# Two of the seven lower parts of a Strassen pair: negated copy and accumulating DMA in place of a VectorE subtraction

## The chip, the cores and the metric

The kernel runs on one core of one Trainium2 chip (trn2). The metric is the device time of one execution in microseconds (us). A core has five engines that run side by side, each with its own queue worked off in order: TensorE (PE in the profile; PEld is its weight load), VectorE (DVE), ScalarE (ACT), GpSimd (POOL) and SyncE (SP), which here only starts DMAs. They wait for one another through semaphores. DMAs move data between the DRAM arrays and the on-chip memory.

## The reference

One inference step of a two-layer encoder over 512 prompt frames and 64 sample frames, model width 1024. Layer 0 mixes tokens by causal pooling, layer 1 by sparse attention; each is followed by a squared-ReLU MLP with 4096 hidden units. All data is float32. What matters here is the MLP:

```python
def _mlp(h, w_up, w_down):
    u = jax.nn.relu(h @ w_up)
    return (u * u) @ w_down
```

It is computed once in each layer, on the 576 frames together.

## The kernel before

**Split weights.** TensorE multiplies in float32r, a shortened float32. To keep accuracy, each weight block is split into an upper part h (the block rounded to float32r) and a lower part l (the block minus h), and each activation likewise; a product is then three matmuls: h by h, h by the activation's lower part, l by h. `split_unit` (L176 to L180) makes a *unit*, the two parts of a block of 128 x 512: ScalarE copies the block into the tile `wh` (L178), VectorE subtracts into `wl` (L179).

**Rings.** Units stand in a ring of six buffers plus, in the MLP, two more (`UNITS`, L39), so eight. The raw blocks come from DRAM by DMAs of 512 KB (`load`, L142 to L145; issued by SyncE in the MLP) into a ring of two plus two buffers (`RAWS`, L41). `loaded` (L182) keeps up to three loads ahead. `next_unit` (L219) makes units up to five ahead of the one that TensorE takes next.

**Stages of an MLP.** The hidden units are worked in four quarters c = 0 to 3. For each quarter there is an up stage (`project`, matmuls at L253, tile `up`), and a down stage. The down stage of a quarter below `strassen` (four quarters in layer 0, three in layer 1) uses a form of Strassen's algorithm with seven products in place of eight: four pairs of output tiles in each of the seven quarters, 28 pairs in all (`Pair`, L387 to L423, tiles `a`, `b`, `c`, matmuls at L384). The last quarter of layer 1 is done without it (tile `dn`).

**A pair's seven half blocks.** Each pair loads two raw blocks, of kinds "even" and "odd"; the even one holds the half blocks a11 and a12, the odd one a21 and a22, each 128 x 512. `made` (L192 to L215) turns them into seven units, in this order: a11; s2 = a21 + a22 + a11; s1 = a21 + a22; a12; a21 + a11; s2 + a12; a22. The sums are made by GpSimd (L205, L206, L210, L213), in place where they can be. So a11, a12 and a22 are split as they come from DRAM; the others exist only on chip. The opening of a pair takes the first three units, the closing the other four; one unit is 12 matmuls. VectorE adds the products to the residual `x` (L409 to L411, L423). In the last Strassen quarter of a layer GpSimd also adds the running sum `g` onto the residual (L414 to L416). The activations' own factors `u` are made by VectorE and ScalarE in `factors` (L363 to L377).

**What sets the order.** Each engine's queue is put in order by a planner that works from its own model of durations and readiness and from the program's order as priority; in the stages around the change nothing is ordered by hand. Waits follow from what an instruction reads and writes, and from a buffer's last readers.

Of the kernel before, what the change touches and what calls it, by code (L numbers as in the profile page):

```python
# [11 lines left out]
AF = mybir.ActivationFunctionType  # L12
ALU = mybir.AluOpType
# [35 lines left out]
def pool_dsa_kernel(ctx: ExitStack, tc: tile.TileContext, a, o):  # L49
    nc = tc.nc  # L50
    act, dve, pool, pe = nc.scalar, nc.vector, nc.gpsimd, nc.tensor
# [11 lines left out]
    def uid(s):  # L63
        count[0] += 1
        return f"{s}_{count[0]}"
# [37 lines left out]
    def f32(t):  # L103
        return t.bitcast(F32)
# [26 lines left out]
    def longer(what, sizes, mlp):  # L131

        if not (mlp and "more" in phase):
            return False
        t, turns[what] = turns[what], turns[what] + 1
        return t * sizes[1] // sum(sizes) != (t + 1) * sizes[1] // sum(sizes)

    def raw_tile(mlp=False):
        pool = phase["more"] if longer("raw", RAWS, mlp) else raws
        return pool.tile([P, 4 * 264], F32, tag="raw", name=uid("raw"))  # L140

    def load(src, n, queue, mlp=False):  # L142
        raw = raw_tile(mlp)
        queue.dma_start(raw[:, :n], src)
        return raw  # L145
# [25 lines left out]
    def unit(n=512, mlp=False):  # L171

        pool = phase["more"] if longer("unit", UNITS, mlp) else weights
        return [pool.tile([P, 528], F32R, tag=t, name=uid(t))[:, :n] for t in ("wh", "wl")]

    def split_unit(src, mlp):  # L176
        h, l = unit(src.shape[1], mlp)
        act.copy(h, src)  # L178
        how["sub"].tensor_tensor(l, src, f32(h), ALU.subtract)  # L179
        return h, l  # L180

    def loaded():  # L182

        waiting = []
        while jobs or waiting:
            while jobs and len(waiting) < LOADS_AHEAD["more" in phase]:
                kind, src, n = jobs.pop(0)
                mlp = kind in MLP_BLOCKS
                waiting.append((kind, load(src, n, nc.sync if mlp else act, mlp)[:, :n], mlp))
            yield waiting.pop(0)  # L190

    def made():  # L192

        blocks = loaded()
        for kind, raw, mlp in blocks:
            if kind != "even":
                n = raw.shape[1] // 2
                for i in range(2):  # L200
                    yield split_unit(raw[:, i * n:(i + 1) * n], mlp)
                continue
            a11, a12, a21, a22 = (t[:, i * 512:(i + 1) * 512] for t in (raw, next(blocks)[1]) for i in range(2))
            s1, s2 = (phase["sums"].tile([P, 512], F32, tag="sum", name=uid("sum")) for _ in range(2))
            pool.tensor_tensor(s1, a21, a22, ALU.add)  # L205
            pool.tensor_tensor(s2, s1, a11, ALU.add)  # L206
            yield split_unit(a11, mlp)
            yield split_unit(s2, mlp)
            yield split_unit(s1, mlp)
            pool.tensor_tensor(a21, a21, a11, ALU.add)  # L210
            yield split_unit(a12, mlp)
            yield split_unit(a21, mlp)
            pool.tensor_tensor(s2, s2, a12, ALU.add)  # L213
            yield split_unit(s2, mlp)
            yield split_unit(a22, mlp)  # L215

    units = made()

    def next_unit(ahead=4, sub=dve):  # L219
# [1039 lines left out]
```

## Time and profile before

| | before |
|---|---|
| median of 3 runs | 1127.58 us (1126.56 to 1128.9) |
| profiled execution, span from first to last instruction | 1125.7 us (its own time; no other figure of it is given) |
| TensorE busy | 1095.9 us (97%), 8254 matmuls |
| VectorE busy | 823.0 us (73%), 1493 instructions |
| ScalarE busy | 537.4 us (48%), 971 instructions |
| GpSimd busy | 336.0 us (30%), 257 instructions |
| DMA traffic | 114.33 MB, 102 GB/s on average |
| TensorE's mean granted clock | 0.987 of full |

The profile is of one execution. A group's row gives line, engine, operation, tiles and shape, the count, then busy us and mean ns of one, and after the second bar the engine's idle time just before and what ended it. A row of a timeline gives the start and the duration in us, and in brackets the idle time before it. A row of waits gives the waiting engine and line, what ended the wait, the total in us, the number of waits and the longest one. Matmuls are pipelined, so a matmul's own duration (295 ns) is longer than the step from one to the next.

### The profile page before, as it was taken

Reading aid. Unit: us, or ns where it says so; the run is one execution under the profiler, and the core shown is the slowest. Engines: PE = TensorE matmul, PEld = TensorE weight load, DVE = VectorE, ACT = ScalarE, POOL = GpSimd, SP = SyncE. Lnnn points to the kernel's source line nnn. Section 1 sums busy time; section 2 is a strip of 40 time slices with the busy share of each in tenths; the row PEclk is TensorE's granted clock in tenths of the full one; section 3 lists DMA queues with packets and bytes.
Section 4 is the critical chain, followed back from the end, with each engine's and each line's share of the span. In section 5 each row is a group of like instructions: output and inputs, shape, how many; then the busy total and the mean of one; then the engine's idle time right before and its main releaser. Section 6 shows DMA issues by size and latency. Waiting matters only on the chain.

```text
span 1125.7 us, 20859 instructions
## 1 busy us (share of the span) xinstructions
PE 1095.9 (97%) x8254; PEld 1083.3 (96%) x8254; DVE 823.0 (73%) x1493; ACT 537.4 (48%) x971; POOL 336.0 (30%) x257
## 2 busy tenths in 40 slices
PE   8999999999999999999799999999999999999995
PEld 8999999999999999999789999999999999999995
DVE  7878857867786797569999944778858867774434
ACT  8544444344434455354387765545434434433431
POOL 3223212403123361157962430023202403350002
PEclk9999999999999999999899999999999999999998
DMA  6221431331232135457632442421331242242202
GB/s 218 97 76 38 115 112 57 95 128 60 76 116 91 39 117 168 131 157 197 178 101 68 134 142 83 145 77 39 113 113 57 90 128 65 59 129 95 76 1 85
DMA packets 47185, 114.33 MB, mean 102 GB/s; under 512 B 8449, under 2 KB 20016, under 8 KB 47088
## 3 DMA queue, kind: packets, MB, share of 16 engines
q1 hardware_dynamic: 42336, 95.66, 27.7%
q10 hardware_dynamic: 4752, 17.34, 4.8%
q8 instruction: 65, 1.06, 0.4%
q14 instruction: 32, 0.26, 0.1%
HBM read 97.90 MB, written 10.89 MB: 97 GB/s over the span
## 4 chain that ended last, share of the span: by engine, by line
PE 90%; DVE 5%; ACT 1%; DMA 1%; issue 1%; POOL 1%; SPq 0%; DVEq 0%; ACTq 0%; POOLq 0%
PE up L253 36%; PE b L384 11%; PE c L384 7%; PE a L384 7%; PE pj L253 7%; PE dn L253 4%; PE o L1015 3%; PE wo L253 3%; PE wa L253 2%; PE sc L976 1%; PE v L809 1%; PE pb L744 1%; PE pt L996 1%; DVE wl L179 1%; DVE work L940 1%; PE o L1019 1%
## 5 line engine op out<-in xcount | busy, mean ns | idle before, releaser
L253 PE MATMUL up<-xs,wh 128*128 128x288 f32 x2048 | 355.2, 295 | 3.9 <-DVE v L355 2.6
L178 ACT CAST wh<-raw 128x512 fp32r<-128x512 f32 (+1 forms) x322 | 197.9, 620 | 300.3 <-PE up L253 115.5
L253 PEld LDWEIGHTS up<-xs,wh 128*128 128x128 f32 x2048 | 299.5, 188 | 5.4 <-DVE v L355 3.5
L179 DVE TENSOR_TENSOR wl<-raw,wh 128x512 fp32r<-128x512 f32 (+1 forms) x298 | 235.2, 792 | 72.7 <-ACT wh L178 67.5
L253 PE MATMUL up<-xs,wl 128*128 128x288 f32 x1024 | 218.7, 295 | 0.0
L205 POOL TENSOR_TENSOR sum<-raw 128x512 f32<-128x512 f32 x28 | 40.7, 1454 | 483.2 <-DMA raw<-in_w_down 406.0
L253 PEld LDWEIGHTS up<-xs,wl 128*128 128x128 f32 x1024 | 164.0, 188 | 0.0
L384 PE MATMUL b<-u,wh 128*128 128x288 f32 x672 | 135.8, 295 | 0.4 <-DVE u L376 0.2
L384 PEld LDWEIGHTS b<-u,wh 128*128 128x128 f32 x672 | 107.5, 188 | 0.8 <-DVE u L376 0.4
L178 ACT CAST wh<-sum 128x512 fp32r<-128x512 f32 x84 | 51.4, 620 | 100.5 <-PE up L253 34.3
L384 PE MATMUL b<-u,wl 128*128 128x288 f32 x336 | 98.8, 295 | 0.0
L384 PE MATMUL a<-u,wh 128*128 128x288 f32 x448 | 92.7, 297 | 2.0 <-DVE u L375 2.0
L355 DVE SCALAR_TENSOR_TENSOR v<-up,rbm 128x576 f32<-128x576 f32 x62 | 46.6, 755 | 65.4 <-PE up L253 64.8
L384 PE MATMUL c<-u,wh 128*128 128x288 f32 x448 | 91.1, 295 | 0.0
L179 DVE TENSOR_TENSOR wl<-sum,wh 128x512 fp32r<-128x512 f32 x84 | 79.9, 955 | 4.8 <-ACT wh L178 3.8
L253 PE MATMUL pj<-xs,wh 128*128 128x288 f32 x448 | 78.9, 295 | 0.0
L384 PEld LDWEIGHTS a<-u,wh 128*128 128x128 f32 x448 | 72.9, 190 | 2.3 <-DVE u L375 2.3
L384 PEld LDWEIGHTS c<-u,wh 128*128 128x128 f32 x448 | 71.9, 188 | 0.0
L253 PEld LDWEIGHTS pj<-xs,wh 128*128 128x128 f32 x448 | 66.6, 188 | 0.7
L384 PE MATMUL a<-u,wl 128*128 128x288 f32 x224 | 66.4, 296 | 0.0
L384 PE MATMUL c<-u,wl 128*128 128x288 f32 x224 | 66.1, 295 | 0.0
L356 ACT ACTIVATE v<-v 128x576 f32<-128x576 f32 x64 | 43.9, 687 | 46.1 <-DVE v L355 45.7
(223 smaller groups left out, 2067.1 us busy)
## 6 DMA issues: line engine op xcount, KB each, us to landing
raw<-in_w_up SPq DMA_DIRECT2D x64, 512.0 KB, 3.5
raw<-in_w_down SPq DMA_DIRECT2D x64, 512.0 KB, 3.5
raw<-in_w_o ACTq DMA_DIRECT2D x16, 512.0 KB, 3.7
raw<-in_w_in ACTq DMA_DIRECT2D x15, 512.0 KB, 3.9
q<-st SPq DMA_DIRECT2D x32, 144.0 KB, 3.3
q<-q SPq DMA_DIRECT2D x16, 256.0 KB, 2.9
x<-in_x SPq DMA_DIRECT2D x8, 288.0 KB, 6.2
xd<-x SPq DMA_DIRECT2D x4, 576.0 KB, 3.0
```

The costliest lines, as they stand in the source:

```text
L178: act.copy(h, src)
L179: how["sub"].tensor_tensor(l, src, f32(h), ALU.subtract)
L205: pool.tensor_tensor(s1, a21, a22, ALU.add)
L253: pe.matmul(pt[h][:, :m] if isinstance(pt, tuple) else pt[:, h, :m], wt, xs[k][:, part, c:c + m], start=(k == 0 and i == 0), stop=(k == n ...
L355: dve.scalar_tensor_tensor(v, pt[:, :, :HT], 0.0, halves(norm.rb), ALU.max, ALU.mult)
L356: act.activation(v, v, AF.Square)
L384: pe.matmul(bank[:, :HT], wt, ut, start=first and j == 0 and i == 0, stop=last and j == 3 and i == 2, skip_group_check=True)
L744: pe.matmul(pt[:, c0:c0 + rhs.shape[1]], lhs, rhs, start=n == 0, stop=n == len(steps) - 1)
L809: pe.matmul(pt[:n, :264], xs[k][:, part, i * P:i * P + n], wt[:, sl], start=(k == 0 and j == 0), stop=(k == KT - 1 and j == 2))
L940: dve.match_replace(wk[:np_], m8[:np_], wk[:np_], TAKEN)
L976: pe.matmul(pt[:, hh, :nw], q[:, 2 * s + hh], ks[g][:, part, :nw], start=part == 0, stop=part == 1)
L1015: pe.matmul(oc[:, 2 * s + hh], pT[:, c:c + P], V[:, kt, vs], start=kt == 0, stop=kt == i)
```

## The change

For a12 and a22 a new function, `split_added`, takes the place of `split_unit`. ScalarE first writes the negated block into `l`, rounded to float32r; that is -h. It then copies the block into `h` as before. GpSimd's queue issues a DMA which reads the same half block from DRAM again and adds it onto `l`, so that l becomes block minus h. VectorE has no part in these two units. For this `loaded` hands the DRAM array along with the raw tile for blocks of kind "even" and "odd". Everything else stays, GpSimd's adds too.

```diff
+    def split_added(src, again, mlp):
+
+        h, l = unit(src.shape[1], mlp)
+        act.activation(l, src, AF.Copy, scale=-1.0)
+        act.copy(h, src)
+        pool.dma_start(l, again, accum_op=ALU.add)
+        return h, l
+
...
-                waiting.append((kind, load(src, n, nc.sync if mlp else act, mlp)[:, :n], mlp))
+                raw = load(src, n, nc.sync if mlp else act, mlp)[:, :n]
+                waiting.append((kind, (src, raw) if kind in ("even", "odd") else raw, mlp))
...
-            a11, a12, a21, a22 = (t[:, i * 512:(i + 1) * 512] for t in (raw, next(blocks)[1]) for i in range(2))
+            (src1, raw1), (src2, raw2) = raw, next(blocks)[1]
+            a11, a12, a21, a22 = (t[:, i * 512:(i + 1) * 512] for t in (raw1, raw2) for i in range(2))
...
-            yield split_unit(a12, mlp)
+            yield split_added(a12, src1[:, 512:], mlp)
             yield split_unit(a21, mlp)
             pool.tensor_tensor(s2, s2, a12, ALU.add)
             yield split_unit(s2, mlp)
-            yield split_unit(a22, mlp)
+            yield split_added(a22, src2[:, 512:], mlp)
```

## The prediction

> **What bounds the kernel now.** I read the page's busy shares first, then the busy time of stretches, the groups, the waits, and last the chain and timelines around the places where TensorE stands still.
>
> ```profile
> span 1125.7 us, 20859 instructions
> ...
> PE 1095.9 (97%) x8254; PEld 1083.3 (96%) x8254; DVE 823.0 (73%) x1493; ACT 537.4 (48%) x971; POOL 336.0 (30%) x257
> ```
>
> TensorE is busy for 1095.9 of 1125.7 us. Only the 29.8 us of idle time, and what they do to its clock, can be won. The change touches the down stages; here are one up stretch and three down stretches (busy us and instruction count of each engine, granted clock, DMA share, GB/s):
>
> ```profile
> core 0: us, PE busy (x) PEld busy (x) DVE busy (x) ACT busy (x) POOL busy (x), PEclk, DMA share, GB/s
> ...
> 387.00:432.00 45.00, 42.77 (x309) 42.30 (x309) 44.64 (x65) 25.30 (x41) 24.55 (x21) 0.96 0.35 117
> ...
> 825.00:875.00 50.00, 50.00 (x380) 50.00 (x379) 36.09 (x48) 23.27 (x32) 10.04 (x7) 1.00 0.23 72
> 875.00:920.00 45.00, 45.00 (x343) 45.00 (x343) 35.47 (x57) 17.16 (x28) 13.01 (x9) 1.00 0.35 108
> ...
> 970.00:1016.00 46.00, 45.85 (x348) 45.62 (x347) 34.75 (x57) 17.89 (x31) 26.32 (x21) 1.00 0.35 109
> ```
>
> An ordinary down stage (875 to 920) has no idle TensorE time at all: 343 matmuls in 45 us, 0.131 us each. VectorE, the engine relieved, has 9.5 us to spare there. So the forecast hangs on two stages: the last one of layer 0 (387 to 432: 2.23 us idle, 309 matmuls where 343 fit, 34 x 0.131 = 4.5 us lost) and the last Strassen one of layer 1 (970 to 1016: 0.15 us). Gains are bounded by 4.6 us; losses are not.
>
> **The change part by part.** Of the splits that VectorE finishes with a subtraction, 28 pairs x 2 = 56 lose it.
>
> ```profile
> L179 DVE TENSOR_TENSOR wl<-raw,wh 128x512 fp32r<-128x512 f32 (+1 forms) x298 | 235.2, 792 | 72.7 <-ACT wh L178 67.5
> ...
> L178 ACT CAST wh<-raw 128x512 fp32r<-128x512 f32 (+1 forms) x322 | 197.9, 620 | 300.3 <-PE up L253 115.5 <-PE b L384 42.3 <-PE c L384 39.7
> ```
>
> VectorE: 56 x 0.79 = 44 us less, none of it under a TensorE wait in an ordinary stage: worth 0 there. ScalarE: 56 x 0.62 = 35 us more, 8 x 0.62 = 5 us a stage on 17 to 25 busy of 45: it costs 0, since its casts sit waiting for a slot to come free (without that cover it would be up to all 35):
>
> ```profile
> ACT wh L178 <- PE b L384: 70.6, 62, 2.6
> ...
> ACT wh L178 <- PE a L384: 50.2, 46, 2.4
> ...
> ACT wh L178 <- PE c L384: 39.7, 43, 1.8
> ```
>
> That is 151 of the 196 down splits: the ring of 6 + 2 units is full, and a split starts when TensorE has let go of the unit eight places back. This gives the lead of a lower part, which decides whether the longer way round is hidden:
>
> ```profile
> 220.56 3.16 PE b L384 x24
> 223.72 1.59 PE c L384 x12
> ```
>
> A unit is 12 matmuls, 1.59 us, so between the release of a slot and the new unit's turn lie 7 x 1.59 = 11.1 us. The new way: ScalarE's negation, 0.62 us; GpSimd's issue of the accumulating DMA; its landing. The trace has neither of the last two. Bounds come from issues on other queues, loads of the same size, and GpSimd's adds:
>
> ```profile
> L144 ACTq DMA_DIRECT2D raw<-in_w_in x15: 334/335/378, 404.0 to 520.6; - x15
> ```
>
> ```profile
> raw<-in_w_down SPq DMA_DIRECT2D x64, 512.0 KB, 3.5
> ...
> x<-in_x SPq DMA_DIRECT2D x8, 288.0 KB, 6.2
> ...
> raw<-in_cache_k SPq DMA_DIRECT2D x4, 256.0 KB, 3.1
> ...
> raw<-in_cache_ki SPq DMA_DIRECT2D x1, 256.0 KB, 2.7
> ```
>
> ```profile
> L213 POOL TENSOR_TENSOR sum<-sum,raw 128x512 f32<-128x512 f32 x28 | 41.0, 1466 | 30.2 <-DVE wl L179 30.2
> ```
>
> Issue: 0.33 us from below, one whole add, 1.47 us, from above; I take 1.0, nearer the add, since the work is GpSimd's own. Landing of 256 KB: 2.7 us from below, 6.2 us (the crowded start of the kernel) from above; I take 4.0, a plain load and some for reading the target. Alone that makes 0.62 + 1.0 + 4.0 = 5.6 us; behind two adds in GpSimd's queue 5.6 + 2.9 = 8.5 us, under 11.1. The upper ends give 0.62 + 1.47 + 6.2 + 2.9 = 11.2 us, a hair over. So: hidden, 0 us; at the upper ends 0.1 us per unit, 56 x 0.1 = 6 us.
>
> GpSimd's queue gets 8 issues a stage, 8 us on 13 busy, 34 of 46 in the last. Each issue first waits for ScalarE's negation; behind it stand the next pair's two sums, a21's sum and L213, and in the last stages L414 to L416, for which VectorE's L423 waits. DMA traffic: 8 x 256 KB in 45 us is 47 GB/s on 108, share 0.35 to about 0.50, or 0.65 if the target is read too: not full. The second reading of the block moves no load's issue on SP.
>
> The raw buffers come free by another engine. SP's queue waits for VectorE's subtractions to issue loads:
>
> ```profile
> SPq L144 <- DVE wl L179: 658.0, 115, 16.3
> ```
>
> For an odd block the last reader becomes ScalarE's copy, 2 x 0.62 = 1.24 us after the slot's release. At the stall this changes almost nothing. ScalarE, VectorE, SP and GpSimd rows just before it, then stretches of 3 us:
>
> ```profile
> 378.96 0.62 ACT L178 CAST wh<-raw 128x512 fp32r<-128x512 f32 x1 [1.33 <-PE up L253]
> ```
>
> ```profile
> 377.67 0.46 DVE L370 TENSOR_TENSOR t<-v 128x288 f32<-128x288 f32 x1 [0.21 <-ACT v L356]
> 379.62 0.69 DVE L179 TENSOR_TENSOR wl<-raw,wh 128x512 fp32r<-128x512 f32 x1 [1.49 <-ACT wh L178]
> ...
> 384.28 1.55 DVE L372 TENSOR_TENSOR t<-v 128x288 f32<-128x288 f32 x1
> 385.75 1.54 DVE L373 TENSOR_TENSOR t<-v,t 128x288 f32<-128x288 f32 x1
> 387.22 2.12 DVE L375 TENSOR_TENSOR u<-v,u 128x864 fp32r<-128x864 f32 x1
> ```
>
> ```profile
> 380.34 16.56 SPq L144 DMA_DIRECT2D raw<-in_w_down  x2
> ```
>
> ```profile
> 383.94 1.58 POOL L205 TENSOR_TENSOR sum<-raw 128x512 f32<-128x512 f32 x1 [14.85 <-DMA raw<-in_w_down]
> ```
>
> ```profile
> 387.00:390.00 3.00, 0.97 (x7) 0.74 (x7) 3.00 (x3) 1.32 (x2) 1.42 (x1) 1.00 0.00 0
> 390.00:393.00 3.00, 2.79 (x14) 2.56 (x13) 3.00 (x6) 2.11 (x4) 1.95 (x2) 0.63 0.00 0
> 393.00:396.00 3.00, 3.00 (x20) 3.00 (x19) 3.00 (x4) 0.62 (x1) 3.00 (x4) 0.80 0.00 0
> ```
>
> TensorE waits for VectorE's factors (L375). These are late because L372 and L373, 1.5 us each where their like (L370) takes 0.46 alone, run beside GpSimd's adds, which begin when a load lands at 383.9; that load goes out at 380.34, when a subtraction ends at 380.31. After the change the buffer is free at 378.96 + 1.24 = 380.20: 0.1 us sooner. Against it, the accumulation of the same block shares the DMA engines with the load and may hold it by up to half of such a load, 1.7 us (512 KB land in 3.5 us). Adds that begin 0 to 1.6 us later let one of VectorE's steps go by undisturbed, up to 1.1 us. I take 0.5 us of gain.
>
> The stall also costs clock: 0.63 and 0.80 granted in the two stretches after it are (0.37 + 0.20) x 3 = 1.7 us lost. The Trainium skill's "TensorE: Matmul & The Clock Gate" (Part 1) has the gate fall back after an idle window of about 3.4 us; the trace has it fall after some 2.2 us idle. By the rule a closed stall would be worth its idle time alone and change the sum by 2.2, by the rows 2.2 + 1.7; the rows decide.
>
> In the last stage of layer 1 the order turns the other way:
>
> ```profile
> 979.92 1.36 ACT L178 CAST wh<-raw 128x512 fp32r<-128x512 f32 x2
> ...
> 997.30 0.62 ACT L178 CAST wh<-raw 128x512 fp32r<-128x512 f32 x1 [1.76 <-PE b L384]
> ```
>
> ```profile
> 982.64 0.68 DVE L179 TENSOR_TENSOR wl<-raw,wh 128x512 fp32r<-128x512 f32 x1
> ...
> 995.06 0.45 DVE L423 TENSOR_TENSOR x<-x,b 128x288 f32<-128x288 f32 x1 [2.47 <-POOL x L415]
> ```
>
> ```profile
> 987.50 1.28 POOL L205 TENSOR_TENSOR sum<-raw 128x512 f32<-128x512 f32 x1 [5.70 <-DMA raw<-in_w_down]
> ...
> 994.22 0.81 POOL L415 TENSOR_TENSOR x<-x,g 128x288 f32<-128x288 f32 x1
> ```
>
> GpSimd works without a break from 987.50 to L415, VectorE waits 2.47 us for it, and TensorE is 0.15 us short. The load that starts the row goes out when the subtraction ends at 983.32; with the copy last, at about 979.92 + 1.36 + 0.62 = 981.9: 1.4 us sooner. An issue placed in the row takes 1.0 of that back. I take 0.1 us of gain.
>
> **Sum.** 0 (ordinary stages) - 0.5 - 0.1 = -0.6 us. The profile's span of 1125.7 us lies 1.9 us under the median of the runs, 1127.58, time outside the span that I leave as it is. A first DMA on GpSimd's queue may have a start of its own, which no row shows; 0 to 1 us, I take 0. Result: 1127.0.
>
> **The rivals.** A: the stall at 387 closes. For it: the adds need only begin some 3 us later, or be placed otherwise by the planner, which gets new costs; and VectorE is relieved. Against: the subtraction saved there stands before the stall, in a time when VectorE waits anyway. It gives 2.2 idle + 1.7 clock: 1127.6 - 3.9 = 1123.7.
>
> B, the other side: GpSimd's queue holds L415. Place: the row from 987 to 995. If the planner puts the issue for that pair's a12 ahead of L415, it stands until ScalarE has negated a12, whose split begins at 997.30 as I read the order of the casts: 997.30 + 0.62 + 1.0 = 998.9 in place of 994.22, 4.7 us late, 3.3 after the sooner start of 1.4. VectorE has no slack there, so beyond the 1.4 every us is TensorE's: 3.3 + 1.7 of clock = 5.0, 1127.6 + 5.0 = 1132.6. The last stage of layer 0 has the same adds and may lose as much again: 1137.6. For it: GpSimd is in order, and at 34 of 46 us the fullest there. Against: L415 is ready sooner than that negation, which a planner sees.
>
> C: the accumulation lands later than the lead allows, over 11.1 - 0.62 - 1.0 - 2.9 = 6.6 us. At 8 us half the 56 units, those behind adds, lose 1.4 us less what the ring then gives back; at 0.7 us each 28 x 0.7 = 20: 1147. For it: reading the target as well; against: no 256 KB load takes half of that.
>
> D: the change does not do what it says, the DMA in effect only trading VectorE's idle time for others' and the planner leaving TensorE's order untouched: 1127.6, no change.
>
> The Trainium skill's "DMA: Bandwidth & Descriptors" (Anatomy of one DMA) puts such a GpSimd DMA at 2.0 us plus its bytes by 436 GB/s; by an estimate from that page 2.6 us for 256 KB, and C would fall away. No run here shows it, and the page says nothing of accumulation's pace.
>
> **How the numbers follow.** Under 0.2%, 2.3 us, this kernel's measurement can't tell a change from none. Forecast 0.40, A 0.25, B 0.20, C 0.10, D 0.05. Faster: A and 0.02 of the forecast, 0.27. Slower: B and C, 0.30. Same: the rest, 0.43. Range: from 1123.0, A with the stage's whole 4.5 us, to 1137.0, the forecast and B at both places (2 x 5.0); it also holds the 6 us of the upper landing. C is left out. The forecast's own range is 1125.5 to 1129.5.
>
> **What would show it.** Right: ordinary down stages with 45 of 45 us busy TensorE, 56 subtractions fewer at L179, POOL idle time ended by ACT before issues, landings under 6.6 us, the stall at 387 still there and within 1 us of its length. A: 340 or more matmuls in 387 to 432 at clock 1.00. B: VectorE's L423 waiting for POOL L415 by over 3 us and TensorE idle behind it. C: TensorE waiting for a DMA on wl in L384. Any TensorE wait for such a landing in an ordinary stage makes the main step, the lead of 11.1 us, wrong.

## The result and the profile after

The changed kernel takes 1134.09 us (median of 4 runs, 1132.63 to 1136.86) against 1127.32 us (1126.56 to 1128.9): 6.8 us slower, ratio 1.0064, 95% interval 1.0046 to 1.0082. The forecast was 1127.0 us in a range of 1123.0 to 1137.0: the time is in the range, but it is slower where no change was forecast. The profiled execution has a span of 1131.5 us, 5.8 more than before; it is one of the quicker of the four.

From the changed kernel's page, the span, the engines' busy time, the DMA queues, the group of the new issues and their landing. Every line number behind L178 is 8 to 10 higher than before (L384 is now L394, L414 to L416 are L424 to L426).

```profile
span 1131.5 us, 21033 instructions
...
PE 1098.1 (97%) x8254; PEld 1084.9 (96%) x8254; DVE 787.2 (70%) x1437; ACT 565.8 (50%) x1027; POOL 381.9 (34%) x313
...
q0 software_dynamic: 8064, 14.68, 7.6%
...
L187 POOL DMA_DIRECT2D wl<-in_w_down x56 | 48.8, 876 | 142.9 <-ACT wl L185 142.6
...
wl<-in_w_down POOLq DMA_DIRECT2D x56, 256.0 KB, 5.0
```

VectorE has 56 instructions fewer and works 36 us less; TensorE has the same 8254 matmuls. An issue holds GpSimd for 0.88 us, and the accumulation lands 5.0 us after the issue begins: the profile counts a landing from the start of the issue.

The changed kernel's busy time by stretch, columns as before (the ordinary stage of layer 1, the last of layer 0, the last Strassen stage of layer 1):

```profile
387.00:432.00 45.00, 41.15 (x295) 40.68 (x296) 41.81 (x57) 26.37 (x44) 27.83 (x27) 0.96 0.59 152
...
875.00:920.00 45.00, 45.00 (x343) 45.00 (x342) 32.26 (x52) 21.07 (x35) 18.73 (x16) 1.00 0.62 149
970.00:1016.00 46.00, 43.74 (x317) 43.31 (x317) 29.55 (x47) 19.52 (x33) 31.35 (x28) 0.96 0.57 133
```

The ordinary stage is as full as before: 343 matmuls, 45.00 of 45 us. Layer 0's last quarter has 295 matmuls in place of 309, layer 1's 317 in place of 348. At 0.131 us each that is 1.8 + 4.1 = 5.9 us, and the spans differ by 5.8: the difference lies in these two quarters. TensorE's waits in the two (waiting engine and line, releaser, total us, number, longest):

```profile
PE a L394 <- DVE u L385: 2.0, 1, 2.0
PE a L394 <- DMA wl<-in_w_down: 1.1, 1, 1.1
PE c L394 <- DVE x L433: 0.8, 1, 0.8
```

```profile
PE a L394 <- DMA wl<-in_w_down: 2.3, 1, 2.3
```

The first line is the old stall at 387 us, unchanged. New are two waits for an accumulation, 1.1 and 2.3 us, and one of 0.8 us for VectorE. Behind the wait of 2.3 us the clock is at half for 3.4 us, 1.7 us lost (the stretch's clock of 0.96 is that: 0.04 x 46 = 1.8). The two stretches in which it falls, columns as before:

```profile
989.00:992.00 3.00, 2.31 (x10) 2.31 (x11) 0.00 (x0) 0.00 (x0) 1.90 (x2) 0.66 0.93 251
992.00:995.00 3.00, 3.00 (x20) 3.00 (x19) 2.07 (x3) 1.24 (x2) 3.00 (x3) 0.77 0.07 29
```

2.3 + 1.7 = 4.0 is layer 1's loss, 1.1 + 0.8 = 1.9 layer 0's.

**Why the accumulation is late.** ScalarE and GpSimd of the changed kernel ahead of the wait of 2.3 us, and the end of it on the chain and on TensorE:

```profile
975.97 0.62 ACT L186 CAST wh<-raw 128x512 fp32r<-128x512 f32 x1
976.49 0.62 ACT L185 ACTIVATE wl<-raw 128x512 fp32r<-128x512 f32 x1
...
982.20 0.62 ACT L178 CAST wh<-sum 128x512 fp32r<-128x512 f32 x1 [4.26 <-POOL sum L223]
```

```profile
974.11 1.29 POOL L215 TENSOR_TENSOR sum<-raw 128x512 f32<-128x512 f32 x1 [3.08 <-DMA raw<-in_w_down]
975.47 1.31 POOL L216 TENSOR_TENSOR sum<-sum,raw 128x512 f32<-128x512 f32 x1
976.72 1.76 POOL L220 TENSOR_TENSOR raw<-raw,raw 128x512 f32<-128x512 f32 x1
978.44 1.26 POOL L426 TENSOR_TENSOR x<-x,g 128x288 f32<-128x288 f32 x1
979.66 1.25 POOL L424 TENSOR_TENSOR x<-x,g 128x288 f32<-128x288 f32 x1
980.88 1.29 POOL L223 TENSOR_TENSOR sum<-sum,raw 128x512 f32<-128x512 f32 x1
982.13 0.81 POOL L425 TENSOR_TENSOR x<-x,g 128x288 f32<-128x288 f32 x1
982.88 0.86 POOL L187 DMA_DIRECT2D wl<-in_w_down  x1
```

```profile
982.88 6.77 DMA wl<-in_w_down
```

```profile
989.70 0.41 PE L394 MATMUL a<-u,wl 128*128 128x288 f32 x1 [2.26 <-DMA wl<-in_w_down]
```

ScalarE has negated a12 at 977.1 (the planner put the negation behind the copy). GpSimd is then in a row of sums and residual additions and comes to the issue at 982.88, 5.8 us later. The sums L215, L216 and L220 in this row are the next pair's: the planner put them ahead of this pair's issue. Landing takes 6.8 us. From the negation's start to the landing: 13.2 us, where the ring gives 11.1.

Why this landing takes 6.8 us and not 5.0 was not tried. SyncE issued two loads of 512 KB beside it, at 982.20 and 984.42:

```profile
982.20 2.56 SPq L144 DMA_DIRECT2D raw<-in_w_down  x2
```

A second accumulation followed at 984.70, but that alone does not do it: in four other places with another accumulation 1.4 to 1.6 us behind, the first lands in 4.0 to 5.2 us.

The same in layer 0's last quarter: the negation ends at 403.97, GpSimd stands before it waiting for the next pair's raw block, then adds four times, and issues at 410.77.

```profile
403.34 0.63 ACT L185 ACTIVATE wl<-raw 128x512 fp32r<-128x512 f32 x1
```

```profile
405.11 1.53 POOL L215 TENSOR_TENSOR sum<-raw 128x512 f32<-128x512 f32 x1 [4.08 <-DMA raw<-in_w_down]
406.61 1.26 POOL L425 TENSOR_TENSOR x<-x,g 128x288 f32<-128x288 f32 x1
407.83 1.29 POOL L216 TENSOR_TENSOR sum<-sum,raw 128x512 f32<-128x512 f32 x1
409.08 1.75 POOL L220 TENSOR_TENSOR raw<-raw,raw 128x512 f32<-128x512 f32 x1
410.77 1.76 POOL L187 DMA_DIRECT2D wl<-in_w_down  x2
```

So the theory tested below, **Q**: the loss is made in GpSimd's queue, where in the last quarters the issue stands behind other work until the lead of 11.1 us is used up. Rivals: **L**, the landing and the DMA traffic (share 0.35 before, 0.6 now) slow the kernel wherever they are; **S**, a fixed cost of GpSimd's first DMA, outside the span. S fell without a kernel of its own: each run of the changed kernel takes 1.7 to 1.8 us beyond its span, and so do the runs of the kernel before (1126.59 us for a span of 1124.8).

### The profile page after: what moved, and what is told of

Its sections match the earlier page's. It is cut to its first block, busy times and chain, and to the rows that moved or that the text cites. A ratio compares the mean times of both kernels' runs of the same rounds, so it can differ in the third digit from the quotient of the medians.

```text
span 1131.5 us, 21033 instructions
## 1 busy us (share of the span) xinstructions
PE 1098.1 (97%) x8254; PEld 1084.9 (96%) x8254; DVE 787.2 (70%) x1437; ACT 565.8 (50%) x1027; POOL 381.9 (34%) x313
## 4 chain that ended last, share of the span: by engine, by line
PE 85%; DVE 5%; DMA 2%; POOL 2%; ACT 2%; issue 2%; SPq 1%; DVEq 0%; POOLq 0%; ACTq 0%
PE up L263 36%; PE b L394 10%; PE a L394 7%; PE c L394 7%; PE dn L263 4%; PE pj L263 3%; PE o L1025 3%; PE wo L263 3%; PE wa L263 2%; PE sc L986 2%; PE pt L1006 1%; PE v L819 1%; PE pb L754 1%; DMA wl<-in_w_down 1%; DVE wl L179 1%
## 5 line engine op out<-in xcount | busy, mean ns | idle before, releaser
L178 ACT CAST wh<-raw 128x512 fp32r<-128x512 f32 (+1 forms) x266 | 163.3, 620 | 248.5 <-PE up L263 106.5
L179 DVE TENSOR_TENSOR wl<-raw,wh 128x512 fp32r<-128x512 f32 (+1 forms) x242 | 193.3, 800 | 76.0 <-ACT wh L178 70.1
L215 POOL TENSOR_TENSOR sum<-raw 128x512 f32<-128x512 f32 x28 | 39.7, 1419 | 329.5 <-DMA raw<-in_w_down 261.1
L394 PE MATMUL b<-u,wh 128*128 128x288 f32 x672 | 136.6, 296 | 0.0
L394 PEld LDWEIGHTS b<-u,wh 128*128 128x128 f32 x672 | 108.4, 189 | 0.2 <-DVE x L433 0.2
L178 ACT CAST wh<-sum 128x512 fp32r<-128x512 f32 x84 | 51.7, 620 | 95.8 <-PE up L263 34.7
L394 PE MATMUL b<-u,wl 128*128 128x288 f32 x336 | 99.4, 296 | 0.0
L187 POOL DMA_DIRECT2D wl<-in_w_down x56 | 48.8, 876 | 142.9 <-ACT wl L185 142.6
L394 PE MATMUL a<-u,wh 128*128 128x288 f32 x448 | 92.4, 299 | 2.0 <-DVE u L385 2.0
L394 PE MATMUL c<-u,wh 128*128 128x288 f32 x448 | 91.3, 296 | 0.8 <-DVE x L433 0.8
L179 DVE TENSOR_TENSOR wl<-sum,wh 128x512 fp32r<-128x512 f32 x84 | 82.4, 981 | 7.9 <-ACT wh L178 5.8
L394 PEld LDWEIGHTS a<-u,wh 128*128 128x128 f32 x448 | 73.0, 191 | 2.3 <-DVE u L385 2.3
L394 PEld LDWEIGHTS c<-u,wh 128*128 128x128 f32 x448 | 72.0, 189 | 1.0 <-DVE x L433 1.0
L394 PE MATMUL a<-u,wl 128*128 128x288 f32 x224 | 67.1, 300 | 3.4 <-DMA wl<-in_w_down 3.4
L394 PE MATMUL c<-u,wl 128*128 128x288 f32 x224 | 66.2, 295 | 0.0
```

Source lines behind the costliest of these rows:

```text
L187: pool.dma_start(l, again, accum_op=ALU.add)
L394: pe.matmul(bank[:, :HT], wt, ut, start=first and j == 0 and i == 0, stop=last and j == 3 and i == 2, skip_group_check=True)
```

## The experiments

**Ordinary quarters alone.** `split_added` only where a pair isn't in a layer's last Strassen quarter:

```diff
-            yield split_added(a12, src1[:, 512:], mlp)
+            yield split_added(a12, src1[:, 512:], mlp) if pair // 4 not in (3, 6) else split_unit(a12, mlp)
```

and for a22 alike; `pair` counts the 28 pairs.

> The change in the five ordinary Strassen quarters alone (20 pairs, 40 accumulations); the last Strassen quarter of each layer splits all seven as before. Theory Q (the loss of 6.8 us comes from the last quarters, where GpSimd's queue reaches the issue 5.8 and 6.8 us after the negation): the loss is gone, 1126.5 to 1128.5 us, no TensorE wait for an accumulation. Rival L (the landing of 5.0 us and the fuller DMA engines slow the kernel wherever they are): 40 of 56 accumulations keep about 5 us of the loss, 1131 to 1133. Rival S (a DMA on GpSimd's queue has a fixed cost of about 1 us outside the span): 1128.3 with the span at 1125.7.

Measured: 1129.2 us, ratio 1.0014 (1.0005 to 1.0022). TensorE's waits of this kernel:

```profile
PE a L396 <- DVE u L387: 2.0, 1, 2.0
PE a L396 <- DMA wl<-in_w_down: 0.8, 2, 0.5
```

Most of the loss is gone, and with it L's 1131 to 1133; but 1.9 us is more than Q allowed, and two short waits for accumulations appeared, in layer 0's third quarter and in layer 1's second. The planner laid this kernel out anew: the two issues stand 4.6 and 4.7 us behind their negations, where the full change had 3.6 and 4.0 in the same places.

**Last quarters alone.** The opposite condition, `pair // 4 in (3, 6)`.

> The change in the last Strassen quarter of each layer alone (8 pairs, 16 accumulations). Q: nearly the whole loss, 1131.5 to 1134.5 us, with TensorE waiting for an accumulation of an a12 in the quarter of layer 1 (2 us and the half clock after it) and in that of layer 0 (about 1 us). L: 16 of 56, 1128.5 to 1130.

Measured: 1131.8 us, ratio 1.0038 (1.0024 to 1.0052). 16 of 56 accumulations make 4.5 of the 6.8 us, so Q; the two waits, 1.6 and 0.7 us, are both in layer 1's quarter, behind issues 5.6 and 8.2 us late. In layer 0's quarter none of the accumulations was late this time, and the clock stayed full behind layer 1's waits, both against what Q said.

**a22 alone, a12 alone.** One of the two lines is set back to `split_unit`.

> The new way for a22 alone in all 28 pairs, a12 as before (28 accumulations). Both of TensorE's waits for an accumulation were for an a12; issues for a22 mostly began 0.3 us after the negation. Q: no such wait, 1126.5 to 1128.5 us. L: half of the loss, 1130 to 1131. S: 1128.3.

Measured: 1128.09 us, ratio 1.0008 (0.9999 to 1.0017): no change that can be told from none, no wait for an accumulation.

> The new way for a12 alone. Theory Q: a12's issues are the ones that stand behind sums, so most of the loss stays, 1130.5 to 1134 us, with TensorE waiting for accumulations whose way takes over 11.1 us; with a22's 28 issues gone from the queue, somewhat less than with both. Rival L: half of the loss, 1130.

Measured: 1134.27 us, ratio 1.0059 (1.0044 to 1.0074): the whole loss with half the accumulations, where Q expected somewhat less. One wait, with the half clock behind it, makes 4.7 of the 7.2 us by which this profile is longer than the one before:

```profile
PE a L394 <- DMA wl<-in_w_down: 2.9, 1, 2.9
```

Another 1.6 us are lost in layer 0's last quarter, where TensorE waits for no accumulation but has three short waits for VectorE's additions (0.2, 0.2 and 0.3 us); these were not followed further.

This pair tells Q from L most sharply: the same number of DMAs of the same size, 0.8 us against 7.1. What differs is what stands ahead of them: in the full change the issue of an a22 begins 0.3 us after the negation in nearly every pair, that of an a12 often behind a pair's sums.

**The residual additions off GpSimd's queue.** In the changed kernel L424 to L426 go to VectorE:

```diff
-                    pool.tensor_tensor(self.hi[0], self.hi[0], g, ALU.add)
+                    dve.tensor_tensor(self.hi[0], self.hi[0], g, ALU.add)
```

and the two behind it alike.

> The changed kernel with the running sum's 24 additions onto the residual (L424 to L426) moved from GpSimd to VectorE. Theory Q (late issues in GpSimd's queue): the issue that came 5.8 us after its negation has three adds fewer ahead of it, the whole way falls from 13.2 to under 11.1 us and TensorE no longer waits for it; 1127 to 1130 us. Rival L (the landing itself): the wait stays, 1132 to 1135.

Measured: 1129.18 us, ratio 1.0019 (1.0010 to 1.0027). GpSimd of this kernel at the place of the wait of 2.3 us:

```profile
972.67 1.28 POOL L215 TENSOR_TENSOR sum<-raw 128x512 f32<-128x512 f32 x1 [2.89 <-DMA raw<-in_w_down]
974.03 1.29 POOL L216 TENSOR_TENSOR sum<-sum,raw 128x512 f32<-128x512 f32 x1
975.28 1.51 POOL L220 TENSOR_TENSOR raw<-raw,raw 128x512 f32<-128x512 f32 x1
977.42 1.29 POOL L223 TENSOR_TENSOR sum<-sum,raw 128x512 f32<-128x512 f32 x1 [0.63 <-DVE wl L179]
978.65 0.88 POOL L187 DMA_DIRECT2D wl<-in_w_down  x1
```

Without the three additions the issue comes 2.7 us after the negation, the whole way is 8.6 us and the wait is gone, as Q says. Two short waits stay in ordinary quarters (0.4 and 0.3 us, ways of 11.3 and 11.2 us).

**A plain copy in place of the accumulation.** `pool.dma_start(l, again)`. The addition is left out.

> The changed kernel with the GpSimd DMA as a plain copy; the adding is left out, so these lower parts hold the whole block and the output is another. It measures what accumulating adds to the landing. If it is the reading of the target, the landing falls from 5.0 to 3 to 3.5 us, the ways of 13.2 and 11.8 us to some 11.4 and 10.0, and the time to 1127.5 to 1130. If it is GpSimd's way of issuing, the landing stays at 4.7 to 5.0 and the time at 1132 to 1135.

Measured: 1129.11 us, ratio 1.0021 (1.0009 to 1.0033). The DMA of this kernel (durations of an issue in ns, min/median/max; then its queue's share and its landing; the last answer gives min/median/max of the landings):

```profile
L187 POOL DMA_DIRECT2D wl<-in_w_down x56: 527/567/720, 92.9 to 1005.0; - x56
...
DMA to landing us min/median/max: 2.9/3.9/4.7
```

```profile
q0 software_dynamic: 8064, 14.68, 4.2%
```

The changed kernel has 857/867/1181 ns and 3.9/5.0/7.6 us for the same bytes. So accumulating costs 0.3 us more to issue, 1.1 us more to land and nearly twice the DMA engines' time (7.6% against 4.2%). The 3.9 us lie between the two expectations. What remains against the 2.7 to 3.1 us of a plain load of this size may be GpSimd's way of issuing, or that this copy turns float32 into float32r, which those loads do not; no run tells the two apart. The issues are as late as in the change (4.6 to 5.5 us), but no way is longer than 10.0 us, and TensorE waits for none. Both terms are needed for the loss: a shorter queue (the kernel before this) or a shorter landing removes it.

The long ways of all kernels together, from the start of the negation to the landing, worked out from each trace, with the wait of TensorE that followed:

| kernel | way, us (of it between negation and issue) | wait of TensorE, us |
|---|---|---|
| plain copy | 10.0 (5.1) | none |
| a12 alone | 10.1 (4.4) | none |
| the change, an a22 | 10.1 (2.9) | none |
| **hold2a**, see below | 10.45 (5.8) | none |
| the change | 11.08 (6.5) | none |
| **best**, see below | 11.23 (6.8) | none |
| ordinary quarters | 11.23 (4.6) and 11.43 (4.7) | 0.3 and 0.5 |
| additions on VectorE | 11.24 (4.8) and 11.34 (4.6) | 0.3 and 0.4 |
| the change | 11.75 (6.8) | 1.1 |
| last quarters | 12.26 (5.6) and 13.06 (8.2) | 1.6 and 0.7 |
| the change | 13.16 (5.8) | 2.3 |
| a12 alone | 14.05 (7.5) | 2.9 |

Every way over 11.1 us but one is followed by a wait, and none under it is: the lead of seven units is the bound. The exception is in **best**, where TensorE had waited 0.4 us for VectorE between this negation and its landing, so that the unit's turn came later. The 13.06 likewise costs less since a wait ahead of it had already moved its turn. The way is counted from the negation, which can begin some tenths after the slot's release, so the bound is not sharper than that.

**The stall at 387 us, before.** It was nearly all that this change could have won, so its reading was tried on the kernel before: GpSimd's three sums of that pair held until the last factors stand, by a copy of one element that the first sum overwrites.

```diff
+            if pair == 13:
+                pool.tensor_copy(s1[:, :1], f32(newest["u"][:, 6, 1, :1]))
             pool.tensor_tensor(s1, a21, a22, ALU.add)
```

> The kernel before, with GpSimd's three sums of the second pair of layer 0's last quarter held until VectorE has written the last factors (one more GpSimd copy of one element a partition). It tests the reading of the stall at 387 us: if it comes from VectorE's factor steps running beside GpSimd's adds, it shrinks from 2.0 to under 0.6 us and the clock stays full: 1123 to 1124.5. If the chain of factor steps is itself too long, the stall keeps over 1.3 us: 1126 to 1127.5.

Measured: 1131.83 us, ratio 1.0038 (1.0025 to 1.0052). The factor steps on VectorE, and the stretch of the stall and the one behind it, with the sums held:

```profile
386.34 0.45 DVE L377 TENSOR_TENSOR t<-v 128x288 f32<-128x288 f32 x1
386.71 0.45 DVE L378 TENSOR_TENSOR t<-v,t 128x288 f32<-128x288 f32 x1
387.08 1.05 DVE L380 TENSOR_TENSOR u<-v,u 128x864 fp32r<-128x864 f32 x1
```

```profile
387.00:396.00 9.00, 9.00 (x70) 9.00 (x69) 5.45 (x10) 1.16 (x1) 6.12 (x8) 1.00 0.01 2
396.00:432.00 36.00, 30.20 (x213) 28.22 (x212) 34.47 (x46) 17.67 (x30) 23.71 (x17) 1.00 0.33 109
```

The same two stretches of the kernel before:

```profile
387.00:396.00 9.00, 6.77 (x37) 6.30 (x37) 9.00 (x11) 4.05 (x6) 6.37 (x6) 0.81 0.00 0
396.00:432.00 36.00, 36.00 (x274) 36.00 (x273) 35.64 (x55) 21.24 (x35) 18.17 (x16) 1.00 0.44 147
```

The reading of the stall is right: the steps that took 1.55, 1.54 and 2.12 us beside GpSimd's sums take 0.45, 0.45 and 1.05, the stall is gone and the clock full (70 matmuls for 37). The time forecast with it is not: the second sum comes 9 us later than before (394.36 for 385.59, in an execution that reaches this stage 2 us later), ScalarE's casts wait for it, and 274 matmuls become 213 in the next 36 us. VectorE, busy for 34.5 of these 36 us, leaves the quarter little room to make up for sums held back. Four more versions tried to keep the gain:

```diff
+                pool.tensor_copy(s1[:, :1], newest["t"][:, 3, :1])
```

holds one step less (**hold2**), the same with the new way for a22 alone (**hold2a**), and the full hold with the residual additions on VectorE, with (**best**) and without (**best0**) the new way for a22.

> The kernel before with GpSimd's three sums of that second pair held one step less: until VectorE's last difference t is written, not until the factors are. The two factor steps left beside the sums then take some 2 us longer together, the sums start 2 us later than before. If the stall at 387 is the contention alone: 1.0 to 1.4 us of it stay, the clock no longer falls, 1124 to 1126 us. If what the full hold lost (sums and casts late by some 6 us) already comes with 2 us: 1127 to 1130.

> The same hold with the new way for a22 alone in all pairs. If the accumulations for a22 cost nothing and give VectorE room in layer 0's last quarter, at or 1 us under the version without them: 1123.5 to 1126. If they have a cost of their own of about 1 us: 1125 to 1127.5.

> Three edits together: the new way for a22 alone, the running sum's additions on VectorE, and GpSimd's sums of the second pair of layer 0's last quarter held until the last factors are written. The held version closed the stall at 387 us and lost it again where L420 to L422 stood ahead of the next sums in GpSimd's queue; without them the sums follow at once. If that reading holds: 1123 to 1125.5 us. If VectorE, full in that quarter, now comes late instead: 1126 to 1130.

> The kernel before with the last two of these edits alone (additions on VectorE, held sums), no accumulating DMA. If the accumulations give VectorE room that it needs in layer 0's last quarter, it is slower than with them, by 1 to 3 us; if not, the same within 1 us.

Measured: hold2 1129.89 us (1.0028, 1.0018 to 1.0038), hold2a 1130.7 (1.0032, 1.0022 to 1.0043), best 1128.78 (1.0019, 1.0010 to 1.0028), best0 1134.39 (1.0065, 1.0052 to 1.0077). In all four the stall at 387 shrinks to 0.6 us or nothing and comes back as waits for VectorE between 393 and 421 us. None beats the kernel before: hold2 and best came out in the second of their two ranges, hold2a above both of its own, and best0 by more behind best than the 1 to 3 us expected. One thing came out of it: best and best0 differ by the accumulations for a22 alone, and these are worth 5.6 us there. With twelve more additions VectorE is late in that quarter by itself; then its relief counts. These are best0's waits of TensorE in the quarter, and best's:

```profile
PE a L390 <- DVE g L415: 3.8, 1, 3.8
PE b L390 <- DVE x L429: 1.0, 1, 1.0
```

```profile
PE b L400 <- DVE x L439: 1.3, 2, 1.1
PE c L400 <- DVE x L439: 0.9, 1, 0.9
```

## Why the prediction was wrong

**Right.** The ordinary stages stay full, as forecast, and VectorE's relief is worth nothing there. The lead of 11.1 us holds as a bound, as far as the table shows. An issue was put at 1.0 us and takes 0.88. The DMA share was put at 0.50 to 0.65 and is 0.57 to 0.62. The stall at 387 us was forecast to stay within 1 us of its length; it is 2.04 us for 2.03, so the 0.5 us of gain put there did not come. What makes it, VectorE's steps beside GpSimd's sums, was shown by holding the sums.

**The step that failed: "behind two adds in GpSimd's queue", 2.9 us.** It was a term of the sum of a lower part's way, 0.62 + 1.0 + 4.0 + 2.9 = 8.5 us against 11.1. In the ordinary quarters the time between negation and issue measures at most 4.0 us in the changed kernel, and the way at most 9.5. In the last quarters it measures 5.8, 6.5 and 6.8 us: the queue there holds the next pair's sums, L424 to L426, and a wait for the next pair's raw block ahead of the issue. The prediction named the same sums and additions, but as standing behind the issue; the planner put them ahead. It had also counted the load (34 of 46 us) and drew no longer queue from it.

**Issue and landing, 1.0 + 4.0 us, were right together, in part by luck.** A landing in the profile begins with the issue, so the sum counted the issue twice; what has to be compared with its 5.0 us is the 5.0 us measured at the median. Taken alone the landing was put 1.0 us too short, and the issue counted twice made up for it. In the latest case the two took 6.8 us, 1.8 more. So the late way in layer 1 has 2.9 us more than the sum in the queue and 1.8 us more in the landing (13.2 for 8.5), the one in layer 0 has 3.9 more in the queue and 0.7 less in the landing (11.75).

With issue and landing at their upper ends and the same 2.9 us of queue the sum came to 11.2, so the loss seemed worth 0.1 us a unit at worst; it is 0 for nearly all units and up to 2.3 us plus the clock for two. That 56 x 0.1 = 6 us lies near the measured 6.8, and that the time lies in the stated range, is luck: the range's upper end was set by B at both places and made to hold these 6 us, and neither is what happened.

**Rival B had the right queue and sign and the wrong direction.** It had the issue hold up L415 and so VectorE; the runs show the additions holding up the issue and so TensorE. That its price for one place, 5.0 us, is near the 4.0 measured is luck. **Rival C had the right symptom**, TensorE waiting for a DMA on `wl`, but put it on the landing alone, spread over 28 units; two units had it.

**The gain at 995 us did not come.** The copy of a22 was to free the raw buffer 1.4 us sooner, and the next pair's first sum with it. That sum began at 990.10 in place of 987.50:

```profile
990.10 1.28 POOL L215 TENSOR_TENSOR sum<-raw 128x512 f32<-128x512 f32 x1 [1.29 <-DMA raw<-in_w_down]
```

Of these 2.6 us, 1.4 are lateness that the execution brings along into layer 1's MLP. The load itself went out at 984.42 in place of 983.35, so against the execution's lateness only 0.3 us sooner: ScalarE's casts ahead of the copy had waited 4.26 us for GpSimd's L223 (the row at 982.20). And it landed after 5.6 us in place of 4.0, beside the two accumulations issued at 982.88 and 984.70. The prediction had this cost, up to 1.7 us for a load that shares the DMA engines with an accumulation, and counted it at 387 us alone.

**The relief of VectorE** was put at 44 us and is 36. The subtractions from raw blocks take 41.9 us less (235.2 before, 193.3 after), those from a sum 2.5 us more; the rest was not followed. Of the latter the shortest and the median are no slower, the longest is: subtractions from a sum before, and after (min/median/max, ns):

```profile
L179 DVE TENSOR_TENSOR wl<-sum,wh x84: 676/692/1773, 84.7 to 1002.6; 128x512 fp32r<-128x512 f32 x84
```

```profile
L179 DVE TENSOR_TENSOR wl<-sum,wh x84: 678/693/2900, 84.1 to 1006.2; 128x512 fp32r<-128x512 f32 x84
```

That one of 2.9 us runs beside an addition and a sum that GpSimd does right behind an issue, at 396 us, and the wait of 0.8 us for L433 follows it.

**Open.** The kernels whose late accumulations are gone or short still take 1.9 to 2.3 us more than before (ordinary 1.9, additions on VectorE 2.3, plain copy 2.2). In the first two the waits for accumulations are 0.8 us of idle time, and by the starts of the matmuls the quarters that hold them are 1.5 and 1.3 us longer than before; the third has no such wait. The plain copy's profile has more idle time and half clock where attention begins (a wait of 2.4 us for 1.3, the clock at half for 13.7 us for 10.2, which is 1.7 us), a stretch that the change doesn't touch and in which a22 alone gained 1.1 us; the planner lays out each kernel anew. Whether that accounts for all of it was not tried. A longer ring, which would test the lead directly, was not tried either.

## What to carry to other kernels

Work that goes from a relieved engine to another one's queue has to be checked in the fullest stage of the taker, not at its mean: count what stands ahead of the new instruction there, waits for loads included, and don't take it that a planner keeps the order in which the program is written. Compare the whole way, queue and landing, with the lead that the ring of buffers gives (units ahead times the time of one); under it the way is free, over it each us is the bound engine's, and in these runs a wait of about 2 us cost its clock as well. If the engine that is to be relieved isn't what the bound engine waits for, look for the price alone.

## What the runs showed of the hardware

An accumulating DMA of 256 KB from DRAM onto a float32r tile takes GpSimd 0.87 us to issue and lands 5.0 us after the issue begins, at the median; a copy from the same queue onto the same tiles takes 0.57 and 3.9, against 2.7 to 3.1 us for a plain load of this size on SyncE's queue. Of the seven accumulations in the changed kernel that were issued 0.6 to 1.8 us behind another, six landed in 6.0 to 7.6 us and one in 5.1. The Trainium skill's "DMA: Bandwidth & Descriptors" (Anatomy of one DMA) would give a GpSimd DMA of this size 2.6 us by an estimate from its fit; the runs differ (3.9 us for the copy, 5.0 for the accumulation).

In the MLP stages of these kernels TensorE's clock fell to half for 3.4 us or more at every single wait of 1.9 us or longer, and stayed full through single waits of up to 1.6 us. The length of one wait is not the whole rule: at 18.8 us of the kernel before it fell where the longest wait nearby was 0.5 us. Two close together are uncertain: 1.0 and 1.3 us (last quarters alone) made it fall, 0.9 and 1.5 us (the full hold) did not. The full idle window of about 3.4 us that the Trainium skill's "TensorE: Matmul & The Clock Gate" (Part 1) speaks of was not needed.
